# A batched 64x64 matmul: output in 1 KB runs, transposes of bf16 pairs, and a later start for b

## The chip, the cores and the metric

The kernel runs on one core of one Trainium2 chip. The metric is the device time in microseconds of one execution; lower is better. A core has five engines with queues of their own (TensorE for matmuls, VectorE, ScalarE, GpSimd, SyncE) and 16 DMA engines that move data between the chip's memory (HBM) and the core's on-chip memories. SBUF is the on-chip memory, PSUM the one that TensorE writes; both have 128 partitions.

## The reference

1,024 independent products of 64x64 matrices in float32:

```python
def setup_inputs():
    return {
        "a": np.random.randn(1024, 64, 64).astype(np.float32),
        "b": np.random.randn(1024, 64, 64).astype(np.float32),
    }

def reference(a, b):
    return np.matmul(a, b).astype(np.float32)
```

Each of a, b and the output is 16.78 MB.

## The kernel before

The batch is cut into 16 tiles t of 64 products, and, for a, into 8 tiles s of 128 products. A tile of b or of the output is 1 MB, one of a is 2 MB in HBM.

**Loads.** `load_a(s)` issues four DMAs (h = 0 to 3) from GpSimd's queue, which cast float32 to bf16 on the way (L65); a partition reads one run of 4 KB. `load_b(t)` issues one DMA of 1 MB in runs of 512 bytes without a cast (L73), from SyncE's queue, but for t = 1 and 3 from ScalarE's. There are three buffers for a and four for b. The first two loads of b wait for a marker, a small memset of the identity matrix that GpSimd runs right after it has issued the first DMA of a.

**From a to weights.** TensorE multiplies the transpose of its stationary operand with the moving one, so a has to be transposed, which TensorE does itself against an identity matrix. `regroup(s)` (VectorE, L88) brings the four pieces of a into one order. `transpose(s, w)` makes 16 transposes of 128x128 bf16 (L97) into two PSUM tiles, which VectorE (L103) and ScalarE (L105) copy to `at_sb`. The columns taken are every second one (`u::2`), so the two values u of the contraction index that lie side by side in a are treated as separate matrices. `spread(t)` (VectorE, L115, four copies of 32 partitions) places the 64x64 blocks, in four bands of 32 partitions, into a block-diagonal tile `at_bd`, of which there are two; its zeros are written once at the start (L177).

**Products.** `cast(t)` (ScalarE, L121) turns b into bf16; for the last t the work is cut in four, shared with VectorE (L126, L128). `multiply(t)` makes 64 matmuls with 128x128 weights and 64 moving columns (L157), into four PSUM tiles of 128x512 float32, and ScalarE copies each to `o_sb` (L169); for the last t VectorE takes two of them (L167). `o_sb` has five buffers.

**Stores.** `store(t)` issues one DMA of 1 MB on GpSimd's queue (L147), for the last t four of 256 KB (L141). With `w=2` in `o_v`, a partition holds two neighbouring rows of a product, so the runs in HBM have 512 bytes.

**Order.** The order in which instructions stand in each engine's queue is that of the program text; engines run in order and wait by semaphores. Loads of a and stores share GpSimd's queue, one behind the other, and each DMA of that queue also waits until the one eight before it has landed. The main loop is

```python
        for t in range(n_t):
            s, half = t // 2, t % 2
            if t + 1 < n_t:
                spread(t + 1)
            if half == 0:
                if s + 2 < n_s:
                    regroup(s + 2)
                if s + 1 + A_AHEAD < n_s:
                    load_a(s + 1 + A_AHEAD)
            multiply(t)
            if t + 1 < n_t:
                cast(t + 1)
            if t + B_AHEAD < n_t:
                load_b(t + B_AHEAD)
```

and after it come one half of the transposes of a later s and the store of t - 1.

Of the kernel before, what the change touches and what calls it, by code (L numbers as in the profile page):

```python
# [6 lines left out]

fp32 = mybir.dt.float32
bf16 = mybir.dt.bfloat16
# [3 lines left out]
def kernel(  # L13
# [9 lines left out]

    nc = tc.nc
    B, M, K = a.shape
    _, _, N = b.shape
# [2 lines left out]
    n_t, n_s = B // 64, B // 128  # L31
    A_AHEAD = 3
    B_AHEAD = 4
    N_BD = 2
# [1 line left out]

    a_v = a.rearrange("(s g h) (mp v) k -> s h g mp (v k)", h=4, g=32, v=16)
    b_v = b.rearrange("(t g h) (kp u) n -> t (h kp) g (u n)", h=4, g=16, u=2)
    o_v = out.rearrange("(t g h) (mo w) n -> t (h mo) g (w n)", h=4, g=16, w=2)

    consts = ctx.enter_context(tc.tile_pool(name="consts", bufs=1))
    a_pool = ctx.enter_context(tc.tile_pool(name="a_pool", bufs=A_AHEAD))
    b_pool = ctx.enter_context(tc.tile_pool(name="b_pool", bufs=B_AHEAD))
    work = ctx.enter_context(tc.tile_pool(name="work", bufs=2))
    o_pool = ctx.enter_context(tc.tile_pool(name="o_pool", bufs=5))
    t_psum = ctx.enter_context(
        tc.tile_pool(name="t_psum", bufs=4, space=bass.MemoryType.PSUM)
    )
    o_psum = ctx.enter_context(
        tc.tile_pool(name="o_psum", bufs=4, space=bass.MemoryType.PSUM)  # L50
    )

    bd_tiles = [
        consts.tile([128, 64, 4, 32], bf16, name=f"at_bd{i}") for i in range(N_BD)
    ]
    identity = consts.tile([128, 128], bf16)
    a_tiles, b_tiles, abf_tiles, at_tiles, bbf_tiles = {}, {}, {}, {}, {}
    held, begun = {}, []

    def load_a(s):  # L60
        a_sb = a_pool.tile([128, 4, 16, 64], bf16, name="a_sb")
        for h in range(4):
            if s == 0 and h == 1:
                begun.append(nc.gpsimd.memset(identity[:], 0.0))  # L64
            nc.gpsimd.dma_start(  # L65
                out=a_sb[:, h, :, :].rearrange("p v k -> p (v k)"), in_=a_v[s, h]
            )
        a_tiles[s] = a_sb

    def load_b(t):  # L70
        b_sb = b_pool.tile([128, 16, 128], fp32, name="b_sb")
        queue = nc.scalar if t in (1, 3) else nc.sync
        load = queue.dma_start(out=b_sb[:], in_=b_v[t])  # L73
        if t < 2:
            tc.add_manual_dep(
                load.ins,
                begun[0].ins.name,
                mybir.DependencyInfo(
                    mybir.DependencyClass.Sync, mybir.DependencyReason.DATA
                ),  # L80
                reason="first load of a goes ahead",
            )
        b_tiles[t] = b_sb

    def regroup(s):
        a_sb = a_tiles.pop(s)
        a_bf = work.tile([128, 16, 4, 64], bf16, name="a_bf")
        nc.vector.tensor_copy(a_bf[:], a_sb[:].rearrange("p h v k -> p v h k"))  # L88
        abf_tiles[s] = a_bf
        at_tiles[s] = work.tile([128, 2, 2, 128, 8], bf16, name="at_sb")  # L90

    def transpose(s, w):
        a_cols = abf_tiles[s][:].rearrange("p v h k -> p v (h k)")
        for u in range(2):
            at_ps = t_psum.tile([128, 8, 128], bf16, name="at_ps")
            for vo in range(8):
                nc.tensor.transpose(  # L97
                    at_ps[:, vo, :], a_cols[:, 2 * vo + w, u::2], identity[:]
                )
            dst = at_tiles[s][:, w, u, :, :]  # L100
            src = at_ps[:].rearrange("p vo q -> p q vo")
            if u == 0:
                nc.vector.tensor_copy(dst, src)  # L103
            else:
                nc.scalar.copy(dst, src)  # L105

    def spread(t):
        at_v = at_tiles[t // 2][:].rearrange(
            "p w u (g mp) vo -> p (w u) g (mp vo)", g=32
        )  # L110
        half = slice(16 * (t % 2), 16 * (t % 2) + 16)
        bd_v = bd_tiles[t % N_BD][:].rearrange("p (wu g) h mo -> p wu g h mo", g=16)
        for h in range(4):
            rows = slice(32 * h, 32 * h + 32)
            nc.vector.tensor_copy(bd_v[rows, :, :, h, :], at_v[rows, :, half, :])  # L115

    def cast(t):
        b_bf = work.tile([128, 16, 128], bf16, name="b_bf")
        b_sb = b_tiles.pop(t)
        if t < n_t - 1:  # L120
            nc.scalar.copy(b_bf[:], b_sb[:])  # L121
        else:
            for gq in range(4):
                rows = slice(4 * gq, 4 * gq + 4)
                if gq % 2:
                    nc.vector.tensor_copy(b_bf[:, rows, :], b_sb[:, rows, :])  # L126
                else:
                    nc.scalar.copy(b_bf[:, rows, :], b_sb[:, rows, :])  # L128
        bbf_tiles[t] = b_bf

    def store(t):
        for piece in held.pop(t):
            piece()

    def multiply(t):
        at_bd, b_bf = bd_tiles[t % N_BD], bbf_tiles.pop(t)
        last = t == n_t - 1
        o_sb = o_pool.tile([128, 4, 4, 2, 64], fp32, name="o_sb")

        def put(gq):  # L140
            nc.gpsimd.dma_start(  # L141
                out=o_v[t, :, 4 * gq : 4 * gq + 4, :],
                in_=o_sb[:, gq, :, :, :].rearrange("p g w n -> p (g w n)"),
            )

        def put_all():
            nc.gpsimd.dma_start(  # L147
                out=o_v[t], in_=o_sb[:].rearrange("p q g w n -> p (q g w n)")
            )

        for gq in range(4):
            o_ps = o_psum.tile([128, 4, 2, 64], fp32, name="o_ps")
            for g4 in range(4):
                g = 4 * gq + g4
                for w in range(2):
                    for u in range(2):
                        nc.tensor.matmul(  # L157
                            o_ps[:, g4, w, :],
                            at_bd[:, (2 * w + u) * 16 + g, :, :].rearrange(
                                "p h mo -> p (h mo)"  # L160
                            ),
                            b_bf[:, g, 64 * u : 64 * u + 64],
                            start=(u == 0),
                            stop=(u == 1),
                        )
            if last and gq % 2:
                nc.vector.tensor_copy(o_sb[:, gq, :, :, :], o_ps[:])  # L167
            else:
                nc.scalar.copy(o_sb[:, gq, :, :, :], o_ps[:])  # L169
        held[t] = [lambda q=q: put(q) for q in range(4)] if last else [put_all]  # L170

    with tc.manual_schedule():
        load_a(0)
        for t in range(B_AHEAD):
            load_b(t)
        for bd in bd_tiles:
            nc.vector.memset(bd[:], 0.0)  # L177
        nc.gpsimd.affine_select(  # L178
            out=identity[:],
            in_=identity[:],  # L180
            compare_op=mybir.AluOpType.not_equal,
            fill=1.0,
            base=0,
            pattern=[[-1, 128]],
            channel_multiplier=1,
        )
        for s in range(1, A_AHEAD):
            load_a(s)
        regroup(0)
        transpose(0, 0)  # L190
        transpose(0, 1)
        spread(0)
        cast(0)
        regroup(1)
        load_a(A_AHEAD)
        transpose(1, 0)
        for t in range(n_t):
            s, half = t // 2, t % 2
            if t + 1 < n_t:
                spread(t + 1)  # L200
            if half == 0:
                if s + 2 < n_s:
                    regroup(s + 2)
                if s + 1 + A_AHEAD < n_s:
                    load_a(s + 1 + A_AHEAD)
            multiply(t)
            if t + 1 < n_t:
                cast(t + 1)
            if t + B_AHEAD < n_t:
                load_b(t + B_AHEAD)  # L210
            if half == 0 and s + 1 < n_s:
                transpose(s + 1, 1)
            if half == 1 and s + 2 < n_s:
                transpose(s + 2, 0)
            if t >= HOLD - 1:
                store(t - HOLD + 1)
        for t in range(n_t - HOLD + 1, n_t):
            store(t)
# [30 lines left out]
```

## Time and profile before

| | |
|---|---|
| median of 11 runs | 138.83 us (138.48 to 139.99) |
| the profiled execution | 138.97 us, span from first to last instruction 137.2 us |
| VectorE busy | 85.8 us (63%) |
| ScalarE busy | 77.3 us (56%) |
| TensorE busy, matmuls | 59.0 us (43%), mean granted clock 0.82 |
| GpSimd busy | 43.1 us (31%) |
| read from HBM, written to it | 33.55 MB, 16.78 MB |

Shares of one engine are means over the span. In the rows of the profile a line has the code's line number (L88), the engine, the operation, what is written and read, the shape, how often it ran, the busy time with the mean time of one in ns, and the time that the engine stood idle before it with what ended it. PE is TensorE, PEld its weight loads, DVE is VectorE, ACT is ScalarE, POOL is GpSimd, SP is SyncE. q0 is the DMA queue that GpSimd fills, q1 SyncE's and q10 ScalarE's.

### The profile page before, as it was taken

The numbers are of one execution on the slowest core, as the hardware profiler recorded it, in microseconds if no ns is written. First come the engines' busy times: TensorE is split into PE (matmuls) and PEld (weight loads), VectorE is DVE, ScalarE is ACT, GpSimd is POOL, SyncE is SP. The second block draws the span as 40 slices with busy tenths as digits, with TensorE's granted clock in tenths as the row PEclk, the third lists the DMA queues.
The fourth block names the chain that finished last, engine by engine and source line by source line (L and its number), as shares of the span: only waits on it lengthen the run. The fifth ranks groups of instructions, "written<-read, shape, count | busy, mean of one in ns | idle before, by whom it ended". The sixth has DMA issues, their size and how long they took to land.

```text
span 137.2 us, 2995 instructions
## 1 busy us (share of the span) xinstructions
PE 59.0 (43%) x1280; PEld 56.8 (41%) x1280; DVE 85.8 (63%) x94; ACT 77.3 (56%) x98; POOL 43.1 (31%) x57
## 2 busy tenths in 40 slices
PE   0000900865359845771077800955029544509000
PEld 0000900865259744670077700955029544509000
DVE  5773573663999899999357950799108948812100
ACT  0130280299728999950979219790497999714000
POOL 6933113322615531333122543330030332133500
PEclk9999995599955999999555995599955999995955
DMA  2999999999999999999999999999999999999992
GB/s 17 187 305 306 306 306 306 297 271 263 252 274 266 311 363 277 274 346 382 352 270 272 373 378 333 268 292 377 382 383 381 378 381 385 379 383 352 295 277 87
DMA packets 17469, 42.14 MB, mean 307 GB/s; under 512 B 1072, under 2 KB 1072, under 8 KB 17456
## 3 DMA queue, kind: packets, MB, share of 16 engines
q0 software_dynamic: 9008, 25.17, 66.9%
q1 hardware_dynamic: 7392, 14.68, 30.3%
q10 hardware_dynamic: 1056, 2.10, 3.9%
q8 instruction: 10, 0.16, 0.5%
q14 instruction: 3, 0.02, 0.0%
HBM read 33.55 MB, written 16.78 MB: 367 GB/s over the span
## 4 chain that ended last, share of the span: by engine, by line
DMA 52%; issue 24%; POOL 8%; DVE 4%; PE 3%; ACT 1%; POOLq 1%; DVEq 0%
DMA a_sb<-in_a_dram 38%; DMA out_dram<-o_sb 14%; POOL out_dram L147 5%; PE o_ps L157 3%; DVE at_bd L115 2%; POOL out_dram L141 2%; ACT b_bf L121 1%; POOL a_sb L65 1%; DVE a_bf L88 1%; DVE at_sb L103 1%; POOLq L244 1%; POOL identity L64 0%; POOLq L147 0%; POOLq L141 0%; DVEq L88 0%
## 5 line engine op out<-in xcount | busy, mean ns | idle before, releaser
L115 DVE COPY at_bd<-at_sb 32x2048 bf16<-32x2048 bf16 x64 | 47.4, 741 | 20.1 <-ACT at_sb L105 19.1
L157 PE MATMUL o_ps<-b_bf,at_bd 128*128 128x64 bf16 x1024 | 40.1, 208 | 45.6 <-ACT b_bf L121 34.3
L157 PEld LDWEIGHTS <-at_bd 128*128 128x128 bf16 x1024 | 39.4, 108 | 47.3 <-issue 33.5
L169 ACT COPY o_sb<-o_ps 128x512 f32<-128x512 f32 x62 | 33.4, 617 | 26.0 <-DMA out_dram<-o_sb 16.6
L65 POOL DMA_DIRECT2D a_sb<-in_a_dram x32 | 20.6, 656 | 41.1 <-DMA a_sb<-in_a_dram 30.6
L147 POOL DMA_DIRECT2D out_dram<-o_sb x15 | 19.0, 1264 | 40.0 <-ACT o_sb L169 27.9
L97 PE MATMUL at_ps<-identity,a_bf 128*128 128x128 bf16 x256 | 21.1, 250 | 22.2 <-DVE a_bf L88 22.2
L121 ACT CAST b_bf<-b_sb 128x2048 bf16<-128x2048 f32 x15 | 29.2, 1944 | 0.0
L97 PEld LDWEIGHTS <-a_bf 128*128 128x128 bf16 x256 | 18.5, 114 | 22.6 <-DVE a_bf L88 22.6
L105 ACT COPY at_sb<-at_ps 128x1024 bf16<-128x1024 bf16 x16 | 16.8, 1049 | 12.7 <-PE at_ps L97 12.7
L103 DVE COPY at_sb<-at_ps 128x1024 bf16<-128x1024 bf16 x16 | 19.5, 1221 | 4.5 <-PE at_ps L97 4.4
L88 DVE COPY a_bf<-a_sb 128x4096 bf16<-128x4096 bf16 x8 | 10.4, 1294 | 9.0 <-DMA a_sb<-in_a_dram 8.8
L177 DVE MEMSET at_bd<- 128x4096 uint32 x2 | 6.9, 3472 | 2.5 <-PEq L233 1.7
L141 POOL DMA_DIRECT2D out_dram<-o_sb x4 | 3.0, 753 | 4.2 <-ACT o_sb L169 3.9
L105 ACT ACT_TABLE_LOAD x1 | 1.3, 1283 | 4.8 <-issue 4.8
L167 DVE COPY o_sb<-o_ps 128x512 f32<-128x512 f32 x2 | 1.4, 692 | 2.5 <-PE o_ps L157 2.5
L128 ACT CAST b_bf<-b_sb 128x512 bf16<-128x512 f32 x2 | 1.1, 616 | 2.9 <-DMA b_sb<-in_b_dram 2.9
L126 DVE CAST b_bf<-b_sb 128x512 bf16<-128x512 f32 x2 | 0.8, 422 | 3.2 <-DMA b_sb<-in_b_dram 3.2
L73 ACT MOVE_SHAPE b_sb<-in_b_dram x2 | 0.6, 320 | 3.2 <-POOL identity L64 2.2
L178 POOL TENSOR_SCALAR_AFFINE_SELECT identity<-identity 128x128 bf16<-128x128 bf16 x1 | 0.4, 352 | 0.0
L64 POOL MEMSET identity<- 128x128 bf16 x1 | 0.2, 223 | 0.0
L233 POOL MEMSET const-float32-0.0<- 128x1 f32 x1 | 0.1, 98 | 0.2 <-issue 0.2
(3 smaller groups left out, 0.3 us busy)
## 6 DMA issues: line engine op xcount, KB each, us to landing
out_dram<-o_sb POOLq DMA_DIRECT2D x15, 1024.0 KB, 21.1
a_sb<-in_a_dram POOLq DMA_DIRECT2D x32, 256.0 KB, 18.0
out_dram<-o_sb POOLq DMA_DIRECT2D x4, 256.0 KB, 8.2
b_sb<-in_b_dram SPq DMA_DIRECT2D x14, 0.5 KB, 20.7
b_sb<-in_b_dram ACTq DMA_DIRECT2D x2, 0.5 KB, 19.9
```

Of the source, the lines that this page charges most:

```text
L65: nc.gpsimd.dma_start(out=a_sb[:, h, :, :].rearrange("p v k -> p (v k)"), in_=a_v[s, h])
L88: nc.vector.tensor_copy(a_bf[:], a_sb[:].rearrange("p h v k -> p v h k"))
L97: nc.tensor.transpose(at_ps[:, vo, :], a_cols[:, 2 * vo + w, u::2], identity[:])
L103: nc.vector.tensor_copy(dst, src)
L105: nc.scalar.copy(dst, src)
L115: nc.vector.tensor_copy(bd_v[rows, :, :, h, :], at_v[rows, :, half, :])
L121: nc.scalar.copy(b_bf[:], b_sb[:])
L141: nc.gpsimd.dma_start(out=o_v[t, :, 4 * gq : 4 * gq + 4, :], in_=o_sb[:, gq, :, :, :].rearrange("p g w n -> p (g w n)"),)
L147: nc.gpsimd.dma_start(out=o_v[t], in_=o_sb[:].rearrange("p q g w n -> p (q g w n)"))
L157: nc.tensor.matmul(o_ps[:, g4, w, :], at_bd[:, (2 * w + u) * 16 + g, :, :].rearrange("p h mo -> p (h mo)"), b_bf[:, g, 64 * u : 64 * u + 6 ...
L169: nc.scalar.copy(o_sb[:, gq, :, :, :], o_ps[:])
L177: nc.vector.memset(bd[:], 0.0)
```

## The change

The change has four parts.

- Output: `o_v` is cut so that a partition holds four neighbouring rows (`w=4`), runs of 1 KB. A product's rows then lie on 16 partitions, not 32. What TensorE leaves in 128 PSUM partitions has to move to others, so each half of a tile t (a PSUM tile of 128x1024 float32, two banks, one buffer for each half) goes out in four copies of 64 partitions and 512 elements. ScalarE does half 0, VectorE half 1. The last t uses four smaller PSUM tiles from the pool of the transposes, each evacuated in four copies of 64x256, by ScalarE and VectorE in turn. `o_sb` has six buffers.
- Transposes: `a_bf` is read as float32, so that two neighbouring bf16 values move as one 4-byte element; 8 transposes per call instead of 16. ScalarE alone copies the results, and `at_sb` and `at_bd` are float32 tiles. The matmuls read `at_bd` as bf16 again, every second element (`c u`, fixed u).
- Start: the first two loads of b wait until the second DMA of a has landed. The identity is made by a library function after the four DMAs of the first a tile; the second `at_bd` is zeroed by GpSimd, after the issue of three tiles of a. ScalarE's queue also issues the loads of b for t = 5 and 7.
- Order: `cast(t + 1)` and `load_b(t + 4)` stand before `regroup` and `multiply(t)`.

```diff
-    o_v = out.rearrange("(t g h) (mo w) n -> t (h mo) g (w n)", h=4, g=16, w=2)
+    o_v = out.rearrange("(t gh x) (mo w) n -> t (x mo) gh (w n)", gh=8, x=8, w=4)
-    o_pool = ctx.enter_context(tc.tile_pool(name="o_pool", bufs=5))
+    o_pool = ctx.enter_context(tc.tile_pool(name="o_pool", bufs=6))
...
-        tc.tile_pool(name="o_psum", bufs=4, space=bass.MemoryType.PSUM)
+        tc.tile_pool(name="o_psum", bufs=2, space=bass.MemoryType.PSUM)
...
-        consts.tile([128, 64, 4, 32], bf16, name=f"at_bd{i}") for i in range(N_BD)
+        consts.tile([128, 2, 16, 2, 4, 16], fp32, name=f"at_bd{i}") for i in range(N_BD)
     ]
-    identity = consts.tile([128, 128], bf16)
+    identity = consts.tile([128, 128], fp32)
...
-            if s == 0 and h == 1:
-                begun.append(nc.gpsimd.memset(identity[:], 0.0))
-            nc.gpsimd.dma_start(
+            load = nc.gpsimd.dma_start(
                 out=a_sb[:, h, :, :].rearrange("p v k -> p (v k)"), in_=a_v[s, h]
             )
+            if s == 0:
+                first_a.append(load)
...
-        queue = nc.scalar if t in (1, 3) else nc.sync
+        queue = nc.scalar if t in (1, 3, 5, 7) else nc.sync
         load = queue.dma_start(out=b_sb[:], in_=b_v[t])
         if t < 2:
             tc.add_manual_dep(
                 load.ins,
-                begun[0].ins.name,
+                first_a[1].ins.name,
...
-    def transpose(s, w):
-        a_cols = abf_tiles[s][:].rearrange("p v h k -> p v (h k)")
-        for u in range(2):
-            at_ps = t_psum.tile([128, 8, 128], bf16, name="at_ps")
-            for vo in range(8):
+    def transpose(s, j):
+        a_cols = abf_tiles[s][:].rearrange("p v h k -> p v (h k)").bitcast(fp32)
+        for wl in range(2):
+            at_ps = t_psum.tile([128, 4, 128], fp32, name="at_ps")
+            for vo in range(4):
                 nc.tensor.transpose(
-                    at_ps[:, vo, :], a_cols[:, 2 * vo + w, u::2], identity[:]
+                    at_ps[:, vo, :], a_cols[:, 4 * vo + 2 * j + wl, :], identity[:]
                 )
-            dst = at_tiles[s][:, w, u, :, :]
-            src = at_ps[:].rearrange("p vo q -> p q vo")
-            if u == 0:
-                nc.vector.tensor_copy(dst, src)
-            else:
-                nc.scalar.copy(dst, src)
+            nc.scalar.copy(
+                at_tiles[s][:, j, :, wl, :, :],
+                at_ps[:].rearrange("p vo (g mp) -> p g mp vo", mp=4),
+            )
...
+            nc.vector.tensor_copy(
+                bd[rows, :, :, :, h, :].rearrange("p j g wl mo -> p j (g wl) mo"),
+                at_tiles[t // 2][rows, :, half, :, :, :].rearrange(
+                    "p j g wl mp vo -> p j (g wl) (mp vo)"
+                ),
+            )
...
+        at_bd = bd_tiles[t % N_BD][:].rearrange("p j g wl h mo -> p j g (wl h mo)")
+        at_bd = at_bd.bitcast(bf16).rearrange("p j g (c u) -> p j g c u", u=2)
...
+        def evacuate(o_ps, gh, n, copy):
+
+            for par in range(2):
+                for wl in range(2):
+                    src = o_ps[64 * wl : 64 * wl + 64, :, par, :, :]
+                    dst = o_sb[64 * par : 64 * par + 64, gh : gh + n, :, wl, :]
+                    copy(dst, src)
+
+        for half in range(2):
+            if not last:
+                o_ps = o_psum.tile([128, 4, 2, 2, 64], fp32, name="o_ps")
+            for g8 in range(8):
+                if last and g8 % 4 == 0:
+                    o_ps = t_psum.tile([128, 2, 2, 2, 64], fp32, name="at_ps")
+                g = 8 * half + g8
+                gl = (g8 % 4 if last else g8) // 2
+                for j in range(2):
                     for u in range(2):
                         nc.tensor.matmul(
-                            o_ps[:, g4, w, :],
...
+                            o_ps[:, gl, g % 2, j, :],
+                            at_bd[:, j, g, :, u],
                             b_bf[:, g, 64 * u : 64 * u + 64],
...
+                if last and g8 % 4 == 3:
+                    copy = nc.scalar.copy if g8 == 3 else nc.vector.tensor_copy
+                    evacuate(o_ps, g // 4 * 2, 2, copy)
+            if not last:
+                copy = nc.vector.tensor_copy if half else nc.scalar.copy
+                evacuate(o_ps, 4 * half, 4, copy)
...
-        for bd in bd_tiles:
-            nc.vector.memset(bd[:], 0.0)
...
+        nc.vector.memset(bd_tiles[0][:], 0.0)
+        make_identity(nc, identity)
         for s in range(1, A_AHEAD):
             load_a(s)
+        nc.gpsimd.memset(bd_tiles[1][:], 0.0)
...
             if t + 1 < n_t:
                 spread(t + 1)
+                cast(t + 1)
+            if t + B_AHEAD < n_t:
+                load_b(t + B_AHEAD)
             if half == 0:
...
             multiply(t)
-            if t + 1 < n_t:
-                cast(t + 1)
-            if t + B_AHEAD < n_t:
-                load_b(t + B_AHEAD)
```

## The prediction

> **What bounds the kernel now.** I read the page's slices first, then the DMA queues by window, then the waits of the engines. The slices of the span, 3.43 us each:
>
> ```profile
> DMA  2999999999999999999999999999999999999992
> GB/s 17 187 305 306 306 306 306 297 271 263 252 274 266 311 363 277 274 346 382 352 270 272 373 378 333 268 292 377 382 383 381 378 381 385 379 383 352 295 277 87
> ```
>
> The 16 DMA engines are busy from slice 1 to the last, while no compute engine is over 63% (VectorE). So the time is DMA work divided by 16, plus head and tail. The rate falls twice: a is counted by what it writes (half of what it reads), so 306 in the load stage is no loss, but 295 and 277 at the end are. The queues in 96 to 121 us, when only b loads and stores run (packets, MB, share of 16 engines):
>
> ```profile
> q0 software_dynamic: 1632, 6.28, 67.1%
> q1 hardware_dynamic: 1622, 3.21, 35.0%
> ```
>
> A store packet is 4 KB (1533 of them in 6.28 MB) and took 0.671 x 25 us x 16 / 1533 = 175 ns; a b packet of 2 KB took 89 ns. The two alternate, so b gets a third of the time and half of the stores' bytes. The end, window by window (PE, PEld, DVE, ACT, POOL, clock, DMA share, GB/s):
>
> ```profile
> 122.00:124.00 2.00, 0.46 (x10) 0.46 (x10) 0.76 (x2) 1.13 (x2) 0.00 (x0) 0.71 1.02 384
> 126.00:128.00 2.00, 0.77 (x21) 0.65 (x18) 0.82 (x2) 0.58 (x1) 1.75 (x4) 0.94 1.05 324
> 128.00:130.00 2.00, 0.00 (x0) 0.00 (x0) 0.00 (x0) 0.00 (x0) 0.73 (x1) 0.91 0.96 272
> 130.00:132.00 2.00, 0.00 (x0) 0.00 (x0) 0.00 (x0) 0.00 (x0) 0.00 (x0) 0.50 1.00 277
> ```
>
> b has landed at 122.8 and stores run alone. They keep 384 GB/s for some 3 us and then settle near 275, at a full share: the same packets last longer. In 126 to 133 us the queue moved 2.01 MB at a share of 99.3%, 226 ns per packet.
>
> What the engines could do if DMA were free is in the rows of L115 and its neighbours, and in what they wait for:
>
> ```profile
> L115 DVE COPY at_bd<-at_sb 32x2048 bf16<-32x2048 bf16 x64 | 47.4, 741 | 20.1 <-ACT at_sb L105 19.1
> L169 ACT COPY o_sb<-o_ps 128x512 f32<-128x512 f32 x62 | 33.4, 617 | 26.0 <-DMA out_dram<-o_sb 16.6
> L103 DVE COPY at_sb<-at_ps 128x1024 bf16<-128x1024 bf16 x16 | 19.5, 1221 | 4.5 <-PE at_ps L97 4.4
> L167 DVE COPY o_sb<-o_ps 128x512 f32<-128x512 f32 x2 | 1.4, 692 | 2.5 <-PE o_ps L157 2.5
> ```
>
> ScalarE waits 16.6 us for a store to free an output buffer: compute runs ahead until the five buffers are full. In 45 to 60 us, unblocked, one t takes 4.7 us, where the DMA needs about 7.5.
>
> **What the Trainium skill says.** (1) DMA: Bandwidth & Descriptors, Why small descriptors are slow: each piece costs about 3 cycles over its 32-byte beats, so 512 bytes are 19 cycles, at that page's 850 MHz 22.4 ns, eight of them 179 ns. The trace's 175 ns agrees. (2) VectorE: DVE Perf Modes, the perf-mode tier table: an SBUF copy runs at 4 elements per cycle in bf16 and 2 in fp32, fp32 from PSUM at 1. L115 (2,048 bf16, 692 ns where nothing disturbs it) and L167 (512 fp32 from PSUM, 692 ns) agree; no row shows an fp32 SBUF copy. (3) TensorE: Matmul & The Clock Gate, Weight-path perf modes: weights are read 32 bits at a time, packed or strided. In the trace a stride-2 weight load exists already (L97, u::2): 16 pairs of load and transpose last 1.06 us at full clock, 66 ns each, against 32 ns for the packed ones of L157 (64 in 2.03 us). (4) SBUF — State Buffer, Who interferes with whom: a VectorE copy in a two-port mode and GpSimd exclude each other. L65 takes 1.18 instead of 0.53 us when L88 runs beside it, which agrees.
>
> **Part 1: 1 KB runs.** 16.78 MB are 4,096 store packets, each now four runs instead of eight. By (1) a 1 KB run is 35 cycles: 4 x 35 = 140 against 152, so the packet goes from 175 to an estimated 161 ns. Saved: 4,096 x 14 ns / 16 = 3.6 us of engine time; at the mean share of 1.04 (queue shares of the page add up to 101.6% of the span, over some 133 us of activity) 3.4 us. Bounds: nothing, if the packet and not the run costs; 6 us, if all above 128 beats (151 ns) goes. The descriptors per store halve, so L147's 1264 ns on GpSimd should fall to about 0.95 (1,024 between the 512 of L141 at 753 and the 2,048 of L147); hidden, GpSimd is 31% busy.
>
> **Part 2: half-partition evacuation.** A copy costs its free size, not its partitions. ScalarE keeps its amount: before four of 617 per t, now four 64x512 of 617 for half 0. VectorE gets four at 692 = 2.8 us per t for half 1 and loses L103 (1.22 per t). ScalarE takes the transposes' copies over: four 128x512 at 617 per s instead of two at 1049, +0.2 us per t. Spread moves the same bytes as 1,024 fp32: by (2) 512 cycles again, taken as 741 ns with today's disturbance. VectorE per s (two t): regroup 1.2 + 8 x 0.74 + 8 x 0.70 = 12.7 us, 6.35 per t, against (1.2 + 2.4 + 5.9) / 2 = 4.8 now. That is still below the DMA's 7.5, but the slack is nearly gone. Also, evacuation of half 1 of t = 2s stands behind regroup(s+2), which waits for a(s+2).
>
> The path on VectorE: a(2) lands near 30 us (part 4); regroup(2) and evacuation of 0 end at 34. From there to the last evacuation: 5 more regroups, 14 spreads, 14 full evacuations and the last tile's eight short copies (0.43 each) and two casts (0.42): 6.0 + 41.5 + 39.2 + 3.4 + 0.8 = 91 us, so 125, and 128 to 129 with waits for a(6), a(7) and for output buffers. The last quarter's store needs some 3 us more.
>
> **Part 3: transposes of pairs.** 128 instead of 256, of fp32. Per t 8 instead of 16; each 66 ns (as now) to four times the cold 118 ns, so 0.5 to 3.8 us per t; I take 0.25 each, 2 us. The matmuls read weights at stride 2: 32 to 66 ns per pair at full clock, 2.0 to 4.2 us per t. TensorE then has 4 to 6.2 us per t, under VectorE's 6.35. Half 1 waits for VectorE's evacuation of t-1 (one buffer per half), then has the spread (3 us) as cover: at 2.1 us it is hidden, at half clock it could come 0.8 late.
>
> **Part 4: the start and b.** b(0), b(1) now wait for the landing of a's second piece instead of the memset at 2.0. Landings of pieces 2, 3, 4 show as released issues:
>
> ```profile
> 7.17 0.53 POOL L65 DMA_DIRECT2D a_sb<-in_a_dram  x1 [0.37 <-DMA a_sb<-in_a_dram]
> 9.73 0.53 POOL L65 DMA_DIRECT2D a_sb<-in_a_dram  x1 [2.03 <-DMA a_sb<-in_a_dram]
> 12.48 1.18 POOL L65 DMA_DIRECT2D a_sb<-in_a_dram  x1 [2.22 <-DMA a_sb<-in_a_dram]
> ```
>
> Issued at 2.3, b moved its first packets only after 6 us (in 4 to 6 us its queue has one). So b is issued near 7.2 and starts near 11, a has all engines until then. That wastes nothing: in 4 to 6 us a alone held a share of 1.10. First a complete at 9.5 instead of 12.3; b(0) at 22 instead of 17; later a pieces at 2.75 us each, a(2) near 30 instead of 33. Four b tiles on the ACT queue (two before) mean a third queue until some 57 us, so b gets more of the DMA and, with q1 holding 12 tiles instead of 14, ends near 113 instead of 122.8. ACT issues each in about 0.8 us, when its queue is empty. GpSimd's new memset (4 us, from 223 ns for 128 elements less some 0.1 fixed) stands ahead of a(3), whose place has 8 pieces queued in front; it may hold VectorE up to 4 us near 10 us, before anything depends on it. Casts and loads moved ahead of multiply let b run ahead, no more.
>
> So stores run alone for the last 17 to 20 us instead of 12.5, with some 6 MB left. If the 275 GB/s are a limit on bytes, 5 MB of them cost 18.2 us instead of 12.7 at 395; the kernel before lost 1.7 us to the same. I count half of it: (5.5 - 1.7) / 2 = +1.9.
>
> **Sum.** Before: span 137.2, time of that execution 138.97, 1.8 around it; median 138.83. Faster stores -3.4; longer lone tail +1.9; tail loss partly cured by larger runs, -1.2 (226 to 190 ns on today's 2 MB: 500 x 36 / 16 = 1.1). Together -2.7 to -2.8: span 134.4, time **136.0**. VectorE's path gives a span of 133 to 134, so both ends are near each other, which is why I add nothing for it but widen upwards.
>
> **Rivals.** *A, forecast*: as above, 133 to 138, chance 0.48. *B, the gain is eaten at the end*: the 275 GB/s hold for 1 KB runs too, or the run costs nothing: -3.4 + 3.8 to 0, 138 to 139.5. For it: the rate is flat from 128 to 133 at full share. Against: mixed stores at 250 GB/s never showed it. 0.19. *C, VectorE becomes the bound* and the kernel is slower: place, spread and evacuation in one in-order stream; price, 13 tiles t from 37 us on; it decides from about 6.8 us per t. If the fp32 copy ran at 1 element per cycle (1.22 us), a t costs 6.35 + 1.9 = 8.3, the time 37 + 13 x 8.3 + 6 + 1.8 = 153; if TensorE at half clock makes it late by 0.8 each and transposes another 0.6, 7.5 per t: 37 + 97 + 6 + 1.8 = 142. For it: 12.7 of 15 us are filled, and 0.50 clock appears in the page. Against: every price is a row of today or the skill's. 0.26. *D*: the saving is the full 6 us and no tail is left, 131.5: 0.07.
>
> **Numbers.** A measurement here can tell 0.5% (0.7 us) from no change. A lies below 138.1 but for 0.03; B: half the same, a quarter each side; C is slower. Faster 0.48 - 0.03 + 0.05 + 0.07 = 0.57; same 0.03 + 0.09 = 0.12; slower 0.05 + 0.26 = 0.31. Range 132 to 142.5: D partly, A and B whole, the cheap form of C; about 2 in 10 outside, nearly all of it above. A's own range: 133 to 138.
>
> **What would show it.** Right: store packets near 161 ns beside b, packets of q0 fewer per MB or equal with a smaller share; first a regroup near 9.5; L115's successor near 700 ns; b's last landing near 113; ScalarE's or VectorE's waits for output buffers still there. Wrong: DMA digits under 9 between 35 and 125 us (then C), a lone tail at 275 GB/s (then B), spreads at 1.2 us, TensorE named as releaser of evacuations for most t.

## The result, and the profile after

| | before | after |
|---|---|---|
| median | 138.82 us (47 runs, 138.36 to 140.12) | 137.29 us (12 runs, 136.79 to 138.11) |
| the profiled execution, its span | 138.97, 137.2 us | 137.69, 135.6 us |

The ratio is 0.9884, with a 95% interval of 0.9863 to 0.9904: 1.2% faster. Forecast were 136.0 us; 2.8 us were to go, 1.5 went. The slices of the span, 3.39 us each (a digit is the busy share of the DMA engines in tenths, 9 is 90% or more):

```profile
DMA  1999999999999999999999999999999999997493
GB/s 18 185 203 266 309 305 303 305 312 273 280 305 306 305 393 349 302 272 364 392 357 271 273 389 396 329 266 297 395 401 394 394 396 396 405 399 300 167 320 137
```

Two things differ from before. b is done at 114.5 us and stores then run alone; they hold about 400 GB/s at first (405 and 399 in the slices from 115 to 122 us) and later 320, where before the lone stores soon fell to 295 and 277. And the digits 7 and 4 are new: shortly before the end the DMA engines have nothing to move. The queues in 96 to 113 us, again almost only b loads and stores (packets, MB, share of 16 engines):

```profile
q0 software_dynamic: 1154, 4.46, 67.9%
q1 hardware_dynamic: 1143, 2.26, 34.7%
```

4.46 MB are 1,089 packets of 4 KB: 0.679 x 17 us x 16 / 1,089 = 170 ns, where it was 175. A b packet takes 0.347 x 17 x 16 / 1,104 = 85 ns, where it was 89. Then the end by windows (PE, PEld, DVE, ACT, POOL, clock, DMA share, GB/s); b's last tile landed at 114.5:

```profile
115.00:120.00 5.00, 3.39 (x61) 3.23 (x62) 4.83 (x8) 3.04 (x6) 1.01 (x1) 0.50 1.02 406
122.00:124.00 2.00, 2.00 (x42) 2.00 (x40) 1.94 (x5) 1.27 (x4) 0.00 (x0) 0.50 1.03 393
124.00:126.00 2.00, 1.22 (x23) 1.06 (x20) 1.94 (x4) 1.67 (x5) 0.27 (x1) 0.69 0.33 123
126.00:128.00 2.00, 0.00 (x0) 0.00 (x0) 1.92 (x6) 0.00 (x0) 2.00 (x3) 1.00 0.38 133
128.00:130.00 2.00, 0.00 (x0) 0.00 (x0) 0.69 (x2) 0.00 (x0) 1.46 (x3) 0.66 1.02 332
130.00:132.00 2.00, 0.00 (x0) 0.00 (x0) 0.00 (x0) 0.00 (x0) 0.00 (x0) 0.50 0.99 320
```

From 124 to 128 us the share is 0.33 and 0.38, so 2 x (0.67 + 0.62) = 2.6 us of DMA time are lost, while VectorE is busy for nearly all of it. What it was doing is in its timeline (start, us, instruction, idle time before it):

```profile
92.03 1.67 DVE L113 COPY at_bd<-at_sb 32x1024 f32<-32x1024 f32 x2
96.56 1.23 DVE L91 COPY a_bf<-a_sb 128x4096 bf16<-128x4096 bf16 x1 [2.87 <-DMA a_sb<-in_a_dram]
97.80 2.79 DVE L157 COPY o_sb<-o_ps 64x512 f32<-64x512 f32 x4
...
122.39 2.79 DVE L157 COPY o_sb<-o_ps 64x512 f32<-64x512 f32 x4
125.22 3.49 DVE L157 COPY o_sb<-at_ps 64x256 f32<-64x256 f32 x8
```

and in GpSimd's, which issues the stores:

```profile
118.99 1.37 POOL L146 DMA_DIRECT2D out_dram<-o_sb  x1 [4.58 <-DVE o_sb L157]
125.73 3.01 POOL L146 DMA_DIRECT2D out_dram<-o_sb  x4 [5.38 <-issue]
129.00 0.72 POOL L146 DMA_DIRECT2D out_dram<-o_sb  x1 [0.26 <-DVE o_sb L157]
```

From 97.8 on VectorE does evacuations (L157) and spreads (L113) without a gap, four of each per tile, 5.9 us. A lone store of 1 MB at 400 GB/s takes 2.6 us. The stores of t = 10 to 13, issued between 101 and 119, had landed by 126.1, but that of t = 14 could only be issued at 125.73, half a microsecond after VectorE's evacuation of it. So the end is set by VectorE's order, and 2 MB of stores follow. In that order the evacuation stands behind a regroup (L91) that waited 2.87 us for a's last tile.

The rows for VectorE and ScalarE:

```profile
L113 DVE COPY at_bd<-at_sb 32x1024 f32<-32x1024 f32 x64 | 46.4, 725 | 7.9 <-ACT at_sb L103 6.0
L157 ACT COPY o_sb<-o_ps 64x512 f32<-64x512 f32 x60 | 34.8, 581 | 12.8 <-DMA out_dram<-o_sb 6.7
L157 DVE COPY o_sb<-o_ps 64x512 f32<-64x512 f32 x60 | 41.3, 689 | 1.0
```

The spread as 1,024 fp32 takes what 2,048 bf16 took (725 against 741 ns). A copy of 64 partitions and 512 elements takes what one of 128 partitions took on VectorE (689 against 692 ns). ScalarE waits 6.7 us for stores, where it was 16.6: compute no longer runs as far ahead.

### The profile page after: what moved, and what is told of

The parts are those of the page before. It is cut to its first block, busy times and chain, and to the rows that moved or that the text cites. A ratio compares the mean times of both kernels' runs of the same rounds, so it can differ in the third digit from the quotient of the medians.

```text
span 135.6 us, 2815 instructions
## 1 busy us (share of the span) xinstructions
PE 68.7 (51%) x1152; PEld 63.8 (47%) x1152; DVE 105.1 (77%) x143; ACT 84.6 (62%) x122; POOL 44.0 (32%) x58
## 4 chain that ended last, share of the span: by engine, by line
DMA 65%; DVE 18%; issue 9%; POOL 3%; POOLq 1%; DVEq 0%
DMA a_sb<-in_a_dram 48%; DMA out_dram<-o_sb 17%; DVE o_sb L157 10%; DVE at_bd L113 8%; POOL out_dram L146 2%; POOL a_sb L66 1%; POOLq L250 1%; DVE a_bf L91 0%; DVEq L91 0%; POOLq L146 0%; DVEq L113 0%; POOLq L239 0%
## 5 line engine op out<-in xcount | busy, mean ns | idle before, releaser
L169 PEld LDWEIGHTS <-at_bd 128*128 128x128 bf16 x1024 | 43.8, 114 | 43.5 <-DVE o_sb L157 33.2
L169 PE MATMUL o_ps<-b_bf,at_bd 128*128 128x64 bf16 x960 | 42.9, 215 | 38.0 <-DVE o_sb L157 30.8
L113 DVE COPY at_bd<-at_sb 32x1024 f32<-32x1024 f32 x64 | 46.4, 725 | 7.9 <-ACT at_sb L103 6.0
L157 ACT COPY o_sb<-o_ps 64x512 f32<-64x512 f32 x60 | 34.8, 581 | 12.8 <-DMA out_dram<-o_sb 6.7
L157 DVE COPY o_sb<-o_ps 64x512 f32<-64x512 f32 x60 | 41.3, 689 | 1.0
L100 PE MATMUL at_ps<-identity,a_bf 128*128 128x128 f32 x128 | 25.4, 367 | 17.3 <-DVE a_bf L91 17.3
L100 PEld LDWEIGHTS at_ps<-identity,a_bf 128*128 128x128 f32 x128 | 21.1, 194 | 17.7 <-issue 17.7
L103 ACT COPY at_sb<-at_ps 128x512 f32<-128x512 f32 x32 | 17.6, 590 | 4.8 <-PE at_ps L100 4.5
L91 DVE COPY a_bf<-a_sb 128x4096 bf16<-128x4096 bf16 x8 | 9.8, 1227 | 12.9 <-DMA a_sb<-in_a_dram 12.8
L157 ACT COPY o_sb<-at_ps 64x256 f32<-64x256 f32 x8 | 2.9, 367 | 3.0 <-PE at_ps L169 2.9
L191 DVE MEMSET at_bd<- 128x4096 f32 x1 | 3.5, 3472 | 1.7 <-PEq L239 1.7
L169 PE MATMUL at_ps<-b_bf,at_bd 128*128 128x64 bf16 x64 | 3.6, 242 | 1.2 <-DVE at_bd L113 1.2
L195 POOL MEMSET at_bd<- 128x4096 f32 x1 | 3.5, 3532 | 0.0
L157 DVE COPY o_sb<-at_ps 64x256 f32<-64x256 f32 x8 | 3.4, 422 | 0.1
```

The costliest lines, as they stand in the source:

```text
L100: nc.tensor.transpose(at_ps[:, vo, :], a_cols[:, 4 * vo + 2 * j + wl, :], identity[:])
L103: nc.scalar.copy(at_tiles[s][:, j, :, wl, :, :], at_ps[:].rearrange("p vo (g mp) -> p g mp vo", mp=4),)
L113: nc.vector.tensor_copy(bd[rows, :, :, :, h, :].rearrange("p j g wl mo -> p j (g wl) mo"), at_tiles[t // 2][rows, :, half, :, :, :].rearrange(
L169: nc.tensor.matmul(o_ps[:, gl, g % 2, j, :], at_bd[:, j, g, :, u], b_bf[:, g, 64 * u : 64 * u + 64], start=(u == 0), stop=(u == 1),)
L191: nc.vector.memset(bd_tiles[0][:], 0.0)
L195: nc.gpsimd.memset(bd_tiles[1][:], 0.0)
```

## The experiments

The theory from the two traces, V: the DMA path is as forecast, near a span of 134, but VectorE's in-order chain ends too late for it. The rival, D (not the prediction's rival D): the stream of the DMA engines sets the end. What is missing is then the saving itself, since stores, above all stores alone, are slower than forecast, and an earlier VectorE would only wait for them. Each expectation says in its own words what the theories give. Ratios are to the kernel before.

**e1: VectorE freed by order.** The evacuation no longer stands behind the regroup that waits for a.

```diff
-                if s + 2 < n_s:
-                    regroup(s + 2)
...
             multiply(t)
+            if half == 0 and s + 2 < n_s:
+                regroup(s + 2)
```

> The kernel after with regroup(s+2) placed behind multiply(t), so that VectorE's evacuation of half 1 no longer stands behind a copy that waits for a. Theory V (VectorE's in-order chain sets the end, it stood 2.9 us at the regroup that waits for the last tile of a): the last VectorE copy comes 1.5 to 3 us earlier than 128.7 us and the time falls from 137.3 to between 134.5 and 136. Theory D (the DMA stream sets the end, VectorE merely finishes with it): 137.0 to 137.6, no change.

Measured: 135.87 us, ratio 0.9788 (0.9755 to 0.982). VectorE's timeline and the slices of e1:

```profile
93.75 2.80 DVE L157 COPY o_sb<-o_ps 64x512 f32<-64x512 f32 x4
96.57 1.23 DVE L91 COPY a_bf<-a_sb 128x4096 bf16<-128x4096 bf16 x1
```

```profile
DMA  2999999999999999999999999999999999999991
GB/s 18 179 200 259 309 306 300 306 309 283 273 294 308 305 385 366 311 276 324 399 381 285 268 346 396 372 275 269 369 402 389 393 401 392 407 402 402 331 340 72
```

The regroup starts at the same 96.57, but now the evacuation fills the wait. The store of t = 14 goes out at 122.93 instead of 125.73, and the digits stay at 9:

```profile
122.93 3.00 POOL L146 DMA_DIRECT2D out_dram<-o_sb  x4 [5.38 <-issue]
```

The span is 133.7, 1.9 us less than in the changed kernel; for the DMA alone 134.4 had been forecast. Theory V holds, and D's "no change" does not.

**e2: VectorE freed by sharing.** Order as in the changed kernel; ScalarE evacuates both halves of three late tiles.

```diff
-                copy = nc.vector.tensor_copy if half else nc.scalar.copy
+                copy = nc.vector.tensor_copy if half and t not in (10, 12, 14) else nc.scalar.copy
```

> The kernel after, with ScalarE evacuating both halves for t = 10, 12 and 14: 3 x 2.8 us leave VectorE's stream and 3 x 2.4 us come to ScalarE's, which was 62% busy. Theory V: the end moves forward by 2 to 5 us, time 132.5 to 135.5, until the DMA engines bind. Theory D: no change, 137.0 to 137.6. If ScalarE becomes late instead: over 137.6.

Measured: 135.40 us, ratio 0.9757 (0.9728 to 0.9785), the fastest version of this study. Its windows, in the same columns:

```profile
122.00:124.00 2.00, 0.05 (x2) 0.00 (x0) 1.92 (x6) 1.93 (x6) 1.22 (x2) 1.00 1.00 393
124.00:126.00 2.00, 0.00 (x0) 0.00 (x0) 0.63 (x2) 0.87 (x3) 1.89 (x4) 0.98 1.00 354
126.00:128.00 2.00, 0.00 (x0) 0.00 (x0) 0.00 (x0) 0.00 (x0) 0.61 (x1) 0.50 1.01 342
128.00:130.00 2.00, 0.00 (x0) 0.00 (x0) 0.00 (x0) 0.00 (x0) 0.00 (x0) 0.50 1.00 348
```

Compute is done by 125, 4 us before the changed kernel's, and the span (133.6) is as in e1, though VectorE ends 1.3 us earlier than there. Beyond that a faster VectorE brings nothing: DMA is the limit again. Most of the half microsecond between the times of e1 and e2 lies outside the span (2.1 us around it in e1 and in the changed kernel, 1.8 in e2 and in the kernel before); no run shows why.

**e3 and e4: the run size alone.** Each store becomes two DMAs of 512 KB. In e3 they split along the half (1 KB runs, the control), in e4 along the row, so that a run has 512 bytes; everything else is the changed kernel. First e3's edit, then e4's:

```diff
-            held[t] = [lambda: put(0, 8)]
+            held[t] = [lambda: put(0, 4), lambda: put(4, 4)]
```

```diff
+        def put_j(j):
+            nc.gpsimd.dma_start(
+                out=o_v[t, :, :, 128 * j : 128 * j + 128],
+                in_=o_sb[:, :, j].rearrange("p gh wl n -> p gh (wl n)"),
+            )
...
-            held[t] = [lambda: put(0, 8)]
+            held[t] = [lambda j=j: put_j(j) for j in range(2)]
```

> The kernel after with each store but the last tile's cut into two DMAs of 512 KB, runs of 1 KB as before: the control for the next run. Both theories: within 0.7 us of 137.3; the queue then holds fewer bytes in its eight DMAs, which could cost up to 2 us.

> As the run before, two DMAs of 512 KB per store, but cut so that each has runs of 512 bytes. The run size alone differs. If the run costs [...]: store packets at 174 instead of 169 ns beside b, 1 to 3.5 us more DMA time before 115 us; if VectorE sets the end, most of it is hidden and the time is within 1 us of its control. If the rate of lone stores depends on the run size, the stores after b fall to about 275 GB/s and the time grows by 2 us or more.

Measured: e3 136.17 us, 0.9811 (0.978 to 0.9843); e4 142.54 us, 1.0266 (1.0235 to 1.0297). First the windows of e3, then of e4:

```profile
115.00:120.00 5.00, 3.78 (x64) 3.47 (x64) 4.83 (x8) 2.68 (x5) 1.68 (x3) 0.50 1.02 403
120.00:125.00 5.00, 3.60 (x64) 3.44 (x64) 4.83 (x9) 2.54 (x7) 0.59 (x2) 0.50 1.02 384
```

```profile
115.00:120.00 5.00, 1.91 (x33) 1.76 (x34) 4.83 (x8) 2.31 (x5) 1.60 (x2) 0.58 1.02 358
120.00:125.00 5.00, 3.51 (x63) 3.35 (x64) 4.83 (x8) 1.97 (x5) 2.34 (x2) 0.50 1.01 287
130.00:135.00 5.00, 0.00 (x0) 0.00 (x0) 0.43 (x1) 0.00 (x0) 2.05 (x3) 0.50 1.00 284
```

While b still comes in (96 to 113 us), the queues of e3, then of e4, are:

```profile
q0 software_dynamic: 1205, 4.41, 67.3%
q1 hardware_dynamic: 1162, 2.29, 35.2%
```

```profile
q0 software_dynamic: 1149, 4.17, 65.8%
q1 hardware_dynamic: 1152, 2.29, 36.7%
```

By the sum used above, a store packet takes 170 ns in e3 and 176 in e4, a b packet 86 and 89: within a nanosecond the figures of the changed kernel and of the kernel before. So the shorter packets of both kinds come from the run size.

The run size is worth 6.4 us in this kernel, more than the whole change. All its other parts together, with 512-byte runs, make a kernel 2.7% slower than before: b is done early (115.9), stores then run alone for 23 us, and alone with short runs they move 287 GB/s. One difference remains between the two: in e3 the first DMA of a tile waits only for ScalarE's half, in e4 each waits for both. It can't carry the 6 us, since e4's DMA share is 0.92 or more in every window from 115 to 135 us, at the low rate. That e3 beats the changed kernel by 1.1 us was not expected (within 0.7); it fits V, as stores become ready in smaller pieces, but no run tests that alone.

**e5 and e6: the start alone.** e5 is the changed kernel with b released by a small memset behind the first DMA of a, as before; e6 is the kernel before with b held until a's second DMA has landed.

The core of e5 (`mark` is a tile of its own), then e6, where the identity matrix is zeroed later, since its memset no longer serves as the marker:

```diff
-            load = nc.gpsimd.dma_start(
+            if s == 0 and h == 1:
+                begun.append(nc.gpsimd.memset(mark[:], 0.0))
+            nc.gpsimd.dma_start(
...
-                first_a[1].ins.name,
+                begun[0].ins.name,
```

```diff
-            if s == 0 and h == 1:
-                begun.append(nc.gpsimd.memset(identity[:], 0.0))
-            nc.gpsimd.dma_start(
+            load = nc.gpsimd.dma_start(
...
+            if s == 0:
+                begun.append(load)
...
-                begun[0].ins.name,
+                begun[1].ins.name,
...
+        nc.gpsimd.memset(identity[:], 0.0)
```

> The kernel after with b's first loads released by a small memset behind the first DMA of a, as in the kernel before. Theory V (VectorE's chain, fed by a, sets the end): a's tiles land 2 to 3 us later, VectorE starts its chain later, time +0.5 to +2 us over 137.3. Theory W (the DMA engines lose nothing at the start either way and the chain is held by later tiles of a): within 0.5 us of 137.3.

> The kernel before with only the start changed: b's first two loads wait for the landing of the second DMA of a. DMA theory: the same bytes at the same share, within 0.5 us of 138.7; b's end moves from 122.8 to some 126 us, so the lone stores of 512 byte runs, at 275 GB/s, get shorter: up to 1 us faster. If the late b holds up compute: slower by 1 us or more.

Measured: e5 139.16 us, ratio 1.0023 (1.0000 to 1.0046), 1.9 us behind the changed kernel. e6 139.80 us, ratio 1.009 (1.0057 to 1.0122), slower than the kernel before. VectorE's first regroup in e5:

```profile
12.33 1.23 DVE L92 COPY a_bf<-a_sb 128x4096 bf16<-128x4096 bf16 x1 [7.20 <-DMA a_sb<-in_a_dram]
```

In the changed kernel it starts at 9.46. VectorE's chain in e5's profile ends 0.7 us later (129.45), and that execution (138.48 us) is 0.8 us over the changed one's; the 22 executions of e5 spread from 138.25 to 140.32, and how the rest of the 1.9 arises in the others isn't seen. The slices of e6:

```profile
DMA  2999999999999999999999999999999999994883
GB/s 21 187 201 270 307 304 305 307 305 272 272 267 300 370 279 271 342 384 350 274 273 376 377 327 268 298 381 379 384 383 375 385 383 380 380 382 180 251 247 114
```

Here the last b lands at 128.9 instead of 122.8; the last tile's cast waits for it and the DMA has nothing else left. (This execution took 141.07 us and is the slowest of seven, so the gap is probably larger in it than in most.) So the late start isn't good or bad in itself: it helps the changed kernel and costs the kernel before. What makes b catch up there is the next experiment; the third queue was not added to the kernel before.

**e7: the third queue alone.** The loads of t = 5 and 7 go back to SyncE's queue.

```diff
-        queue = nc.scalar if t in (1, 3, 5, 7) else nc.sync
+        queue = nc.scalar if t in (1, 3) else nc.sync
```

> The kernel after with b's tiles 5 and 7 on SyncE's queue again (two on ScalarE's instead of four). Then b ends later than 114.5 us, by 4 to 6 us, and a gets more of the DMA engines between 34 and 60 us. Theory V: a's later tiles land earlier, VectorE waits less, time 0.5 to 2 us less than 137.3. Theory D: no change.

Measured: 140.61 us, ratio 1.0122 (1.0091 to 1.0153), 3.3 us behind the changed kernel, which neither theory had. The row of the cast, first of the changed kernel, then of e7, and e7's slices:

```profile
L124 ACT CAST b_bf<-b_sb 128x2048 bf16<-128x2048 f32 x15 | 28.6, 1907 | 7.6 <-DMA b_sb<-in_b_dram 7.6
```

```profile
L124 ACT CAST b_bf<-b_sb 128x2048 bf16<-128x2048 f32 x15 | 28.5, 1901 | 27.7 <-DMA b_sb<-in_b_dram 27.7
DMA  2999999999999999999999999999999999957493
```

In 45 to 60 us b comes in at 2.06 MB / 15 us = 137 GB/s in e7, and at (1.63 + 1.19) / 15 = 188 over two queues in the changed kernel:

```profile
q1 hardware_dynamic: 1036, 2.06, 38.3%
```

```profile
q1 hardware_dynamic: 827, 1.63, 30.8%
q10 hardware_dynamic: 614, 1.19, 21.1%
```

All queues together move 329 GB/s in both. So the second queue for b adds no bandwidth; it gives b a larger part of it. 137 GB/s are a tile in 7.7 us, and from 71 to 110 us e7's casts start 7.6 to 7.8 us apart, each behind a wait for b. So the evacuations come late, and the DMA runs dry at the end as in e6.

**e8: all three remedies.** The regroup late, both halves on ScalarE for t = 12 and 14, and two DMAs per store.

> The kernel after with regroup behind multiply, ScalarE evacuating both halves for t = 12 and 14, and stores of two DMAs with 1 KB runs. If after these nothing but the DMA stream is left: 134.8 to 135.6, no better than each alone by more than 0.6, and no idle DMA before the last landing. If VectorE still bound the runs with one of the edits: under 134.5.

Measured: 135.88 us, ratio 0.9793 (0.9761 to 0.9825), no better than e1 or e2 alone and 0.3 us over the expected range. They cure the same gap; what remains is the stream of the DMA itself.

**e9 and e10: stores alone.** 16 stores of 1 MB from one zeroed tile, with the addresses of the kernel before (e9) and of the changed one (e10). Loads, transposes and products are left out.

> Stores alone: 16 DMAs of 1 MB from one zeroed tile on GpSimd's queue, with the output's addresses in runs of 512 bytes as in the kernel before. The loads of a and b, the transposes and the products are left out, so the output is zeros. If the rate of lone stores is limited per run (or by the half-size writes), the queue settles near 275 GB/s as at the end of the kernel before, packets of 4 KB near 230 ns at a full share, and the 16.8 MB take about 61 us of moving. If the low rate at the end of the kernel before came from loads that had just ended, or from something else of that kernel, the rate is near 380 to 400 GB/s and the moving takes 42 to 44 us.

> The same stores with the addresses of the changed kernel, runs of 1 KB; the same parts are left out and the output is zeros. If the run size sets the lone rate: 345 to 405 GB/s, packets of 4 KB at 160 to 190 ns, 41 to 49 us of moving, 12 to 20 us less than with 512 bytes. If the limit of 275 GB/s is one on bytes that 1 KB runs only reach later than the end of the changed kernel (rival B in a weaker form), it shows here after some us: a high rate for the first 5 to 15 us, then the same 275 GB/s as with 512 bytes, and a total within 5 us of it.

Measured: 73.65 and 60.78 us, one run each. Slices of e9 (1.8 us each), then of e10 (1.5 us each):

```profile
GB/s 0 0 25 287 248 262 267 264 267 267 271 269 264 260 264 271 269 269 267 262 269 269 267 267 260 267 274 267 269 269 258 264 271 276 274 217 196 198 144 9
```

```profile
GB/s 0 0 0 230 308 305 322 330 328 325 333 325 336 328 330 325 328 328 333 325 330 325 330 330 330 330 330 328 328 328 328 330 336 339 339 347 250 203 172 0
```

After the first slices the rate is flat: 267 GB/s with 512-byte runs, 329 with 1 KB. With all 16 engines at a full share that is 4,096 x 16 / 267 = 245 ns and 199 ns per 4 KB packet. The 12.9 us between the two are near the low end of the expected 12 to 20. They differ in the run size and in which rows a partition holds; e4 keeps the rows of e3 and shows the low rate as well (287 and 284 GB/s), so the run size sets it. But 329 is below what was expected (345 to 405) and below the 400 that the changed kernel keeps from 115 to 124 us. From 128 on, and in e2 from 126, it has 320 to 348, near e10's rate.

**e11: b less early.** If mixed traffic moves 396 GB/s and lone stores 329, it should pay to let b end later. This is e2 with three loads of b on ScalarE's queue, as a diff against the changed kernel without e2's own line:

```diff
-        queue = nc.scalar if t in (1, 3, 5, 7) else nc.sync
+        queue = nc.scalar if t in (1, 3, 5) else nc.sync
```

> The kernel of e2 (ScalarE evacuates both halves of t = 10, 12, 14), with three instead of four loads of b on ScalarE's queue, so that b gets less of the DMA early and ends later, near 118 to 119 us, and stores run alone for about 14 us instead of 18. If lone stores settle at 330 GB/s after some us, as the stores alone showed, and mixed traffic holds 395, some 2 MB move from 330 to 395 GB/s: about 1 us less than e2, 134.4, with no wait of compute for b. If compute is fed by b as in e7 (4 loads to 2 cost 3.3 us), half of that comes back: 1.5 us or more slower than e2, near 137, with ScalarE's waits for b between the 8.4 us of e2 and the 27.7 of e7, and DMA digits under 9 near the end. Within 0.4 us of e2 (135.0 to 135.8): both are small here.

Measured: 137.84 us, ratio 0.9932 (0.9906 to 0.9958), 2.4 us behind e2. Its end:

```profile
122.00:124.00 2.00, 2.00 (x42) 2.00 (x40) 1.11 (x3) 1.96 (x4) 0.00 (x0) 0.50 1.00 393
124.00:126.00 2.00, 0.53 (x10) 0.37 (x7) 1.92 (x6) 1.94 (x5) 0.00 (x0) 0.50 0.35 127
126.00:128.00 2.00, 0.00 (x0) 0.00 (x0) 0.35 (x1) 1.93 (x6) 1.21 (x2) 0.50 0.20 72
```

b's last landing moved to 119.9 as meant, but compute is fed later by as much, ScalarE's waits for b rise from 8.4 to 11.8 us, and the DMA runs dry from 124 to 128. Two, three and four tiles on ScalarE's queue give 140.6, 137.8 and 135.4 us (the first without e2's edit): in this kernel an early b is needed, and its price is the longer lone tail.

## Why the prediction was right in direction and 1.3 us off in size

- **Faster stores, -3.4 us: too large.** Store packets beside b take 170 ns, not 161; the saving is 5 to 6 ns instead of 14, or about 1.4 us over 4,096 packets and 16 engines. But a b packet beside them fell from 89 to 85 ns, which was not forecast: by the pages' shares b's two queues took 46.9 us of the 16 engines' time before (34.2% of 137.2) and 46.1 in e1 (34.5% of 133.7). The mixed rate rose from 381 to 396 GB/s, by 3.9%; the forecast packets (161 + 89 against 175 + 89) stood for 5.6%. The estimate from the Trainium skill's DMA: Bandwidth & Descriptors, Why small descriptors are slow (3 cycles per run) is thus too large beside b, and e9 and e10 show it too small for stores alone, where four runs fewer save 46 ns.
- **Longer lone tail, +1.9, and its cure, -1.2: the wrong sign.** Stores ran alone for 19.6 us, as forecast (17 to 20), and the DMA was dry for 2.6 of them. The limit is there, as rival B held, but it depends on the run: 267 GB/s became 329 (199 ns per packet, 190 forecast), and it came only after some 9 us at 400. e1 shows the price where the DMA doesn't run dry: the lone packets averaged 174 ns (6.17 MB at a share of 86.0% over 19.1 us), some 5 more than beside b, 0.5 us in all. Before they averaged 205 (4.01 MB at 83.6% over 15 us), 30 more, 1.8 us. So the two terms together came out at -1.3, not +0.7. The queue of stores and a's loads on the page of before, then of e1:

```profile
q0 software_dynamic: 9008, 25.17, 66.9%
```

```profile
q0 software_dynamic: 9008, 25.17, 66.6%
```

That is 91.8 us of 137.2 and 89.0 of 133.7. The 2.8 us between them are what the sum of -2.7 had, but by luck, as two errors of about 2 us cancel; the 0.8 of b's packets come on top. For DMA alone the forecast span of 134.4 compares with 133.6 to 133.8 in e1, e2 and e3, where the DMA is hardly ever without work.
- **VectorE's path, span 133 to 134: the step that failed.** Its prices were right: 725 ns for a spread, 689 for an evacuation, the last copy at 128.7 after a forecast 128 to 129. The term behind it was not: "The last quarter's store needs some 3 us more." When VectorE ended, not a quarter but 1.6 of the 2.1 MB of t = 14 and 15 were still to be moved, since t = 14 could only go out at 125.73; at 330 GB/s the 2.1 MB take 6.4 us, from about 127.7 to 134.1. So the path ends 5.4 us after VectorE's last copy instead of 3, and the span is 135.6. "I add nothing for it" rested on this: I compared VectorE's 6.35 us per tile with 7.5 us of DMA, which holds while a and b are loaded. Once b has landed the DMA needs 2.6 us per tile, and VectorE is the slower one. e1 and e2 show it: both take away only VectorE's delay and end at the DMA's span. Of the 1.3 us that the time is off, some 0.3 are outside the span, as said under e2.
- **Rival C** named the right engine, yet at prices that did not occur; VectorE decides only at the end, for some 1.9 us of span (135.6 to 133.7). The sign named for it, digits under 9 before 125 us, shows in one slice, from 122.0 to 125.4.
- **The start.** First regroup 9.46 (forecast 9.5), b(0) 22.3 (22), a(2) 28.5 (30), last b 114.5 (113): right. What it is worth was only in the lone tail of the sum; e5 puts it at 1.9 us here, and e6 at a loss of 1.0 in the kernel before.
- **The third queue** was counted as a reason for an early b, and not as a condition. e7 and e11 show compute starving with less.
- **Transposes** took 134 ns at full clock (eight in 1.07 us) and 244 at half clock (eight in 1.95), where 0.25 us had been put; weight pairs at stride 2 took 34.7 ns at full clock (32 in 1.11 us), near the low bound of 32. TensorE waits 30.8 us for VectorE's evacuation and is released late by it, not the reverse; VectorE's evacuations wait 1.0 us in all. The memset on GpSimd took 3.53 us (4) and is not in the chain of work that ended last.

The parts don't add up: with everything else in place, undoing the run size costs 6.4 us, the queues 3.3, the start 1.9, and the whole change brings 1.5. e4 suggests that an early b and short runs hurt each other (23 us of stores alone at the low rate), and e7 that long runs without an early b bring nothing; no run changed these two alone. Left open is what the transposes of pairs and the half-partition copies are worth by themselves; neither was undone alone.

## What to carry to other kernels

Compare engines stage by stage: an engine with 15% of slack beside loads and stores (6.35 us per tile against 7.5) can be twice too slow (5.9 against 2.6) once the loads are done, and the stores that it holds back come on top of its end. Before a change is priced by busy time, ask in which order the engine that gets the new work stands, and what wait is ahead of it in the queue. When loads are moved forward, the last stage becomes stores alone; measure what rate these have by themselves, with the run size that they will have.

## What the hardware showed that was not expected

- Stores alone run slower per packet than the same stores beside loads: 245 against 175 ns with 512-byte runs, 199 against 170 with 1 KB. The DMA share is 1.0 in both, so a full share is no sign of a full rate.
- After the last load the higher rate lasts for a while: about 3 us with 512 bytes in the kernel before, 9 us with 1 KB here (in e2 393 GB/s up to 124 us, then 354 and 342). In e9 and e10, with no loads at all, it never occurs. Why is open.
- Longer runs in the stores made the loads beside them faster: b's packets took 89 ns before and in e4, 85 and 86 in the changed kernel and in e3.
- A transpose of 128x128 fp32 takes just over twice that of bf16 (134 against 66 ns at full clock, 244 against 118 at half), so moving pairs as fp32, with half as many transposes, saved TensorE no time on them.
